# A hybrid decoder layer on one core: a smaller first load, products of ones at the start, a shorter last norm, and another order of work

## The chip, the cores and the metric

The kernel runs on one core of one Trainium2 chip. The metric is device time in microseconds (us); lower is better.

## The reference, cut to what matters

One layer (DEPTH 1), sequence 1024, width 1024, everything in float32. The normalised input goes through one projection to 5,648 columns; three mixers (SSD with 16 heads, HGRN2 with 4 heads, S5 with 32 groups) work on their parts; the three results are joined to 2,048 columns, projected back to 1,024, normalised and added to the input.

```python
h = rms_norm(x, pre_norm_w[l])
proj = h @ w_in[l]
z, xbc, dt_raw, q, f_raw, i_in, g, u, s5_gate = jnp.split(proj, splits, axis=-1)
y_ssd = ssd_mixer(z, xbc, dt_raw, ...)
y_hgrn = hgrn2_mixer(q, f_raw, i_in, g, lb_all[l], hgrn_norm_w[l])
y_s5 = s5_mixer(u, s5_gate, ...)
mix = jnp.concatenate([y_ssd, y_hgrn, y_s5], axis=-1).astype(x.dtype)
x = x + rms_norm(mix @ w_out[l], post_norm_w[l])
```

`rms_norm(y, w)` is `y * rsqrt(mean(y * y) + 1e-6) * w` over a row.

## The kernel before, in words

**Products.** Each float32 operand of a projection is split into a high part in float32r (an ACT copy) and a low part (a subtraction on DVE or POOL); `split` (L369) does both, and `mm3` (L373) makes three products of them. `c3(t)[:, k]` is the k-th block of 128 columns of a tile. A projection tile is 8 blocks x 2 halves of 512 columns x 3 products.

**The start.** `begin` (L445) projects the first two tiles, F0 and Q0, straight from the raw input: the norm's factor is multiplied in afterwards. It loads two weight tiles (`wr`, 128 x 1024) in halves and eight input blocks (`xs[k]`, 128 x 1024). For each block k ACT makes the high part `h`, scaled with column k of `prew`, DVE the low part `l` by a scalar_tensor_tensor; twelve products follow, six for each weight tile; ACT squares the block and DVE adds the square into `acc`. The weights are split in halves of 512 columns, at k = 0 and k = 4. Loads go out on two queues: `WQ` is ACT's, `S` is SyncE's (SP). After the last block two products with `ones` sum the squares, and `side_by_side` (L428) goes on with the next tiles while `normalise` (L507) rewrites `hh` and `hl`.

**The middle.** `PLAN` (L1531) is a string in which each letter emits one stage: `h` a head of HGRN2, `s` and `o` the two parts of an S5 batch, `c` a chunk of the SSD, `u x z a g v d` projections and preparations. The small products of the mixers write to four one-bank PSUM tiles (`c0` to `c3`, taken in turn by `bank()`), the projections mostly to two two-bank tiles (`p0`, `p1`).

**The end.** `s5_glu` (L1150) makes the S5 output and prepares half of the output weights `w_out` (`wout`, L851: an ACT copy scaled with `mix_w`, and a scalar_tensor_tensor on DVE); the eight others, into `r` tiles, follow at L1507. `out_prep` and `out_gate` load and gate a chunk of 128 rows, `out_split` (L1378) splits it into `v` tiles (ACT copy, DVE subtraction), `out_final` (L1385) multiplies with `w_out`, takes the row's sum of squares from an ACT Square with `accum_out`, corrects an approximate reciprocal root by one Newton step on 128 x 1 tiles (`y_`, `z_`, `v_`, `tot`), and writes chunk c. The last chunk is computed in three pieces of 512, 256 and 256 columns, whose sums are added.

**The order.** All instructions are recorded in a book. `Step` (L77) gives each a length in ns and a time after which others see its result (`post`); `depends` (L130) finds who must wait for whom; `arrange` (L169) is a list scheduler over the five engines with a model of the DMA bus (`BYTES` per ns, `TRIP`), of PE's slow clock and tile switches (`SWITCH`), of ACT's tables (`LOAD`) and of the port shared by DVE and POOL; among the ready instructions it takes the one that can start first, then the one of lowest rank, with a malus of `KEEP` for a change of tile kind or table. `improve` (L256) runs it forward and backward six times, each time with the start times of the run before as ranks, and keeps the shortest. `force` (L268) then fixes each engine's sequence, queues included.

Of the kernel before, what the change touches and what calls it, by code (L numbers as in the profile page):

```python
# [1 line left out]

# [13 lines left out]
P = 128  # L16
# [57 lines left out]
TABLES = {AF.Exp: 0, AF.Sigmoid: 1, AF.Silu: 2, AF.Gelu_apprx_tanh: 3, AF.Abs_reciprocal_sqrt: 4}  # L74


class Step:  # L77


    def __init__(self, i, ins):  # L80
        self.i, self.ins, self.mode, self.post, self.port = i, ins, None, 100.0, False
        self.eng = str(ins.engine).split(".")[-1]
        self.dma = ins.opcode == "DMACopy"
        if self.dma:
            o, x = ins.outs[0].bass_ap, ins.ins[0].bass_ap
            n = 1
            for _, c in o.ap:
                n *= int(c)
            run = min(int(y.ap[-1][1]) if int(y.ap[-1][0]) == 1 else 1 for y in (o, x))
            self.bytes = 4 * n / max(min(1.0, run * 4 / 512), 0.05)  # L90
            self.len = 60.0
        elif self.eng == "PE":
            n, t = size(ins.outs[0]), ins.tile_size[1]
            r = str(ins.ins[0].dtype).split(".")[-1] == "float32r"
            self.mode = t
            self.post = 200.0
            self.len = max(n / 2.4 + 14, 40) if r else 109.0 if ins.is_transpose else max(4 * n / 2.4 * t / P + 2, 15)
        else:
            n = max(size(x) for x in list(ins.outs) + list(ins.ins) if hasattr(x, "bass_ap"))
            srcs = [x.bass_ap for x in ins.ins if hasattr(x, "bass_ap")]  # L100
            self.post = 100.0
            if self.eng == "Activation":
                self.len = 140 + n / 1.2 + (80 if len(srcs) > 1 and n < 512 else 0)
                self.mode = TABLES.get(getattr(ins, "func", None))
            elif self.eng == "Pool":
                self.len = 50 + n / 1.15 if ins.opcode == "Memset" else 90 + 2.22 * n
                self.port = ins.opcode != "Memset"
            else:
                big = [x for x in srcs if size_of(x) > 1 or n == 1]
                self.port = not any(str(x.tensor.space) == "PSUM" for x in srcs)  # L110
                self.len = 95 + n / 0.96
                if ins.opcode == "Reciprocal":
                    self.len = 95 + 6.2 * n
                elif getattr(ins, "is_tensor_tensor_scan", False):
                    self.len += 105
                elif ins.opcode == "TensorScalarPtr" and len(big) > 1 and n > 32:
                    self.len += 55
                elif ins.opcode == "TensorScalarPtr" and self.port and n > 32:
                    self.len = 95 + n / 1.7


class Turn:

# [3 lines left out]
        self.i, self.behind = i, set()  # L127


def depends(book, places, rings, turns):  # L130

    steps = [Step(i, x) for i, x in enumerate(book)]
    ring = {n: f"{names[i % 2]} ring" for names in rings for i, n in enumerate(names)}
    banks = {x.bass_ap.tensor.name for b in book for x in b.outs if str(x.bass_ap.tensor.space) == "PSUM"}
    turn = [(set(x), set(y), Turn(len(book) + k)) for k, (x, y) in enumerate(turns)]
    seen = {}
    for s in steps:
# [15 lines left out]
        for (nm, c0, c1), w in ops:  # L155
# [2 lines left out]
                old[:] = [y for y in old if not (c0 <= y[0] and y[1] <= c1)]  # L158
            old.append((c0, c1, w, s.i))
        s.pre.discard(s.i)  # L160
    return steps + [x for *_, x in turn]


SWITCH, LOAD, BYTES, TRIP = 165.0, 1283.0, 255.0, 2000.0

STEP, KEEP, ROUNDS = 130.0, {"PE": 3000.0, "Activation": 3000.0}, 6


def arrange(steps, rank, back=False):  # L169
# [14 lines left out]
    engs = {s.eng: [] for s in steps if s.eng}  # L184
    now, mode, best = dict.fromkeys(engs, 0.0), dict.fromkeys(engs), dict.fromkeys(engs)
    order = {e: [] for e in engs}
    bus, cold, port = 0.0, 0.0, {"DVE": (0.0, 0.0), "Pool": (0.0, 0.0)}
    for s in steps:
        if not left[s.i] and s.eng:
            engs[s.eng].append(s.i)  # L190
# [11 lines left out]
    while any(engs.values()):  # L202
# [6 lines left out]
        order[e].append(i)  # L209
        start[i] = t  # L210
        if s.dma:
            bus = max(t + 1300, bus) + s.bytes / BYTES
            now[e] = t + s.len
            end = bus + TRIP - 1300
        else:
            n = s.len
            if e == "PE":
# [37 lines left out]

def improve(steps, rank):  # L256

    best = None
    for _ in range(ROUNDS):
        order, start, total = arrange(steps, rank)  # L260
        if best is None or total < best[1]:
            best = order, total
        _, start, _ = arrange(steps, start, True)
        rank = start
    return best[0]


def force(tc, steps, order):  # L268
# [8 lines left out]
def trunk(ctx: ExitStack, tc: tile.TileContext, a: dict, out: bass.AP, dbg=None):  # L277
# [124 lines left out]


    with tc.high_priority(offset=2 * PRI):
        prew = load_const("pre_w", [P, KD])
    ones = cst.tile([P, P], F32, tag="ones", name="ones")
    V.memset(ones, 1.0)
    eps = cst.tile([P, 1], F32, tag="eps", name="eps")
    V.memset(eps, EPS)
    warm = cst.tile([P, 1], F32, tag="warm", name="warm")  # L410
    A.copy(warm, ones[:, 0:1])
    hh, hl, xs = [], [], []

    def weights(src):

# [29 lines left out]
    def begin(ms):  # L445

        wr = [get("w") for m in ms]
        for w, m in zip(wr, ms):
            WQ.dma_start(w[:, HS[0]], a["w_in"][m][:, HS[0]])
        for k in range(KD):  # L450
            xs.append(slot())
            if k == 0:
                for n in range(2):
                    S.dma_start(xs[k][:, HS[n]], a["xT"][k][:, HS[n]])
            else:
                S.dma_start(xs[k], a["xT"][k])
            if k == 3:
                for w, m in zip(wr, ms):
                    S.dma_start(w[:, HS[1]], a["w_in"][m][:, HS[1]])
        ws = [[], []]  # L460
        ps = [pair(), pair()]
        acc = slot()
        for k in range(KD):
            h, l = get("r"), get("r")
            hf, i = k // 4, k % 4
            for t in range(2):
                if i == 0:
                    ws[t].append((get("v"), get("v")))
                    split(wr[t][:, HS[hf]], *ws[t][hf], V)
                if t == 0:  # L470
                    for s in HS if k == 0 else [slice(0, L)]:
# [913 lines left out]
    def out_final(c, y, hs, w, postw, parts=None):  # L1385
# [4 lines left out]
        if last:  # L1390
            pieces = [slice(0, 512), slice(512, 768), slice(768, 1024)]
            ps = [ps[0], ring("p")[:, 0:256], bank()[:, 0:256]]
        ms = small([P, 6], "ms")
        xr, o, junk = get("x"), get("x"), get("x")
        S.dma_start(xr, a["x"][c * P:(c + 1) * P, :])
        source, parts = parts or out_split(y, hs), []
# [8 lines left out]
        for i in range(4):  # L1405
            parts.append(next(source) if not isinstance(source, list) else source[i])
            if not last:
                for n in range(2):
                    product(i, n)
                free(*parts[i][:2])  # L1410
        y_, z_, v_ = ms[:, 0:1], ms[:, 1:2], ms[:, 2:3]
        tot = ms[:, 3:4]
        if last:
            for n, cols in enumerate(pieces):
                for i in range(4):
                    product(i, n)
                act(junk[:, cols], ps[n], AF.Square, accum_out=ms[:, 3 + n:4 + n])
                if n > 0:
                    add(V, tot, tot, ms[:, 3 + n:4 + n])
                if n < len(pieces) - 1:  # L1420
                    mul(V, o[:, cols], ps[n], postw[:, cols])
        else:
            act(junk, p, AF.Square, accum_out=tot)
        act(y_, tot, AF.Abs_reciprocal_sqrt, scale=1.0 / D, bias=eps)
        ts(V, v_, tot, 1.0 / D, ALU.mult, EPS, ALU.add)
        if last:
            mul(V, o[:, cols], ps[n], postw[:, cols])
        else:
            mul(V, o, p, postw)
        free(y, hs, junk)  # L1430
        mul(V, z_, y_, y_)
        stt(z_, z_, -0.5, v_, ALU.mult, ALU.mult)
        stt(y_, z_, 1.5, y_, ALU.add, ALU.mult)
        for s in pieces if last else [slice(0, L)]:
            stt(o[:, s], o[:, s], y_, xr[:, s], ALU.mult, ALU.add)
# [84 lines left out]
        parts = None  # L1520
    late_names = kept["s"] + kept["q"] + [postw.tensor.name]
    places = dict(zip(kept["m2"] + late_names, kept["y"] + kept["m"] + kept["y"]))
    steps = depends(book, places, rings.values(), [(kept["y"], kept["m2"]), (kept["m"] + kept["m2"], late_names)])
    force(tc, steps, improve(steps, [-STEP * s.ins.bass_priority if s.eng else 0.0 for s in steps]))


# [78 lines left out]
```

## Time and profile before

| what | us |
|---|---|
| median of 3 runs (lowest, highest) | 879.29 (878.73, 880.14) |
| the profiled execution | 878.0 |
| its span, first to last instruction | 876.2 |
| PE busy in the span | 854.7 |
| DVE, ACT, POOL busy in the span | 574.0, 396.5, 257.2 |

PE is TensorE's product row, PEld its weight loads, which run beside the products. DVE is VectorE, ACT ScalarE, POOL GpSimd, SP SyncE; a q behind a name means its queue, where transfers are issued. A product's end is modelled, so "busy" can hold short gaps: pace is read from the number of products in a stretch. The idle time before an instruction is put down to the event that came last.

### The profile page before, as it was taken

What the parts mean: (1) busy time and instruction counts of PE and PEld (TensorE: products, weight loads), DVE (VectorE), ACT (ScalarE), POOL (GpSimd) and SP (SyncE); (2) the same over time, 40 slices, a digit from 0 to 9 for tenths busy, and PEclk for the clock granted to TensorE, in tenths of its full rate; (3) what the DMA queues carried; (4) which work ended last, traced back from release to release, by engine and by line L of the source; (5) the groups of instructions that cost most, each with busy time, mean ns of one, the idle gap of its engine ahead of it and who ended that gap; (6) DMA issues with size and microseconds to landing.
All of it is one profiled execution on the core that took longest, in us unless ns stands there. A gap on an engine that the chain in (4) does not pass through costs nothing.

```text
span 876.2 us, 14850 instructions
## 1 busy us (share of the span) xinstructions
PE 854.7 (98%) x5857; PEld 704.9 (80%) x5857; DVE 574.0 (66%) x997; ACT 396.5 (45%) x627; POOL 257.2 (29%) x224
## 2 busy tenths in 40 slices
PE   7999999999999999999999999999999999999997
PEld 5789877789888888788888787877887778888886
DVE  6698389995748797767537353278656978555521
ACT  8465154562234525353257883773536732222210
POOL 0365032453233336234212243254113403111000
PEclk9999999999999999999999999999999999999999
DMA  7323012345233423356457595377866935343110
GB/s 269 92 63 133 2 49 74 97 149 150 59 97 83 140 86 109 83 139 202 147 168 227 179 341 165 114 235 231 274 198 166 327 122 190 132 133 132 61 49 25
DMA packets 91750, 124.67 MB, mean 142 GB/s; under 512 B 8416, under 2 KB 64416, under 8 KB 91680
## 3 DMA queue, kind: packets, MB, share of 16 engines
q1 hardware_dynamic: 80592, 99.01, 36.4%
q10 hardware_dynamic: 11088, 24.71, 9.7%
q8 instruction: 46, 0.75, 0.3%
q14 instruction: 24, 0.20, 0.1%
HBM read 89.52 MB, written 34.18 MB: 141 GB/s over the span
## 4 chain that ended last, share of the span: by engine, by line
PE 78%; DVE 12%; issue 3%; DMA 2%; ACT 2%; POOL 2%; SPq 0%; DVEq 0%; POOLq 0%; ACTq 0%
PE p L38 58%; PE c L38 20%; DVE m L38 7%; DVE x L38 2%; DVE h L38 1%; POOL v L38 1%; DMA m<-in_xT 1%; DMA x<-sm_d 1%; ACT r L38 1%; DVE r L38 1%; DVE s L38 1%; DMA w<-in_w_in 1%; DVE v L38 0%; DVE s5ph L38 0%; ACT x L38 0%
## 5 line engine op out<-in xcount | busy, mean ns | idle before, releaser
L38 PE MATMUL p<-r,v 128*128 128x512 f32 (+1 forms) x2208 | 536.0, 396 | 6.0 <-ACT r L38 5.9
L38 PEld LDWEIGHTS p<-r,v 128*128 128x128 f32 x2208 | 407.7, 189 | 93.3 <-issue 6.1
L38 POOL TENSOR_TENSOR v<-w,v 128x512 fp32r<-128x512 f32 x76 | 111.9, 1475 | 265.8 <-ACT v L38 204.8
L38 ACT ACTIVATE v<-w 128x512 fp32r<-128x512 f32 x88 | 54.5, 628 | 164.0 <-PE p L38 159.8
L38 DVE TENSOR_TENSOR m<-m,m 128x512 f32<-128x512 f32 (+8 forms) x114 | 106.2, 956 | 29.9 <-ACT m L38 15.0
L38 PE MATMUL p<-s,v 128*128 128x512 f32 (+1 forms) x384 | 88.8, 388 | 3.2 <-DVE v L38 3.2
L38 PEld LDWEIGHTS p<-s,v 128*128 128x128 f32 x384 | 70.3, 188 | 18.8 <-DVE v L38 4.5
L38 PEld LDWEIGHTS c<-m,m 128*32 128x32 f32 (+2 forms) x1904 | 61.2, 127 | 15.7 <-DVE m L38 7.8
L38 ACT ACT_TABLE_LOAD x53 | 68.0, 1283 | 11.7 <-DVE m L38 4.9
L38 PE MATMUL c<-m,m 128*32 128x16 f32 (+3 forms) x1904 | 66.4, 210 | 2.1 <-DVE m L38 2.0
L38 DVE SCALAR_TENSOR_TENSOR x<-p,conv_w,x 128x1023 f32<-128x1023 f32 (+2 forms) x36 | 46.0, 1277 | 8.5 <-ACT x L38 7.9
L38 PE MATMUL p<-y,r 128*128 128x272 f32 (+1 forms) x384 | 48.5, 286 | 0.8 <-DVE x L38 0.8
L38 PEld LDWEIGHTS p<-y,r 128*128 128x128 f32 x384 | 47.5, 190 | 1.3 <-ACT m L38 1.0
L38 ACT ACTIVATE m<-m,acol 128x128 f32<-128x128 f32 x128 | 40.0, 391 | 8.5 <-DMA m<-na_d 3.2
L38 PE MATMUL c<-s,s 128*128 128x512 f32 x192 | 43.7, 389 | 0.0
L38 PEld LDWEIGHTS c<-s,s 128*128 128x128 f32 x192 | 36.0, 188 | 7.5
L38 DVE TENSOR_TENSOR m<-m,sc 128x1024 f32<-128x1024 f32 x16 | 22.6, 1414 | 25.8 <-ACT m L38 25.3
L38 DVE TENSOR_TENSOR v<-x,v 128x512 fp32r<-128x512 f32 x20 | 15.6, 786 | 34.5 <-ACT v L38 34.5
L38 ACT ACTIVATE v<-x 128x512 fp32r<-128x512 f32 x20 | 12.4, 630 | 55.6 <-PE p L38 49.2
L38 POOL TENSOR_TENSOR h<-h 128x256 f32<-128x256 f32 (+1 forms) x12 | 10.6, 887 | 71.2 <-ACT h L38 50.2
L38 ACT COPY m<-c 128x512 f32<-128x512 f32 (+2 forms) x50 | 21.6, 446 | 19.2 <-PE c L38 19.0
L38 DVE SCALAR_TENSOR_TENSOR r<-m,pre_w,r 128x1024 fp32r<-128x1024 f32 (+1 forms) x17 | 26.4, 1561 | 1.6 <-ACT r L38 1.6
(195 smaller groups left out, 954.1 us busy)
## 6 DMA issues: line engine op xcount, KB each, us to landing
w<-in_w_in ACTq DMA_DIRECT2D x38, 512.0 KB, 3.9
m<-na_d SPq DMA_DIRECT2D x16, 512.0 KB, 5.1
xc_d<-x SPq DMA_DIRECT2D x12, 512.0 KB, 3.3
q<-in_w_out SPq DMA_DIRECT2D x12, 512.0 KB, 4.7
m<-tb_d SPq DMA_DIRECT2D x16, 256.0 KB, 4.5
m<-xc_d SPq DMA_DIRECT2D x8, 512.0 KB, 5.4
zc_d<-x SPq DMA_DIRECT2D x8, 512.0 KB, 5.4
ym_d<-m SPq DMA_DIRECT2D x8, 512.0 KB, 3.7
```

The source lines that it names most:

```text
L38: made = f(*args, **kw)
```

## The change

At the start, the two weight tiles are loaded in three pieces (columns 0 to 127 on ACT's queue, 128 to 511 after block 1, 512 to 1023 after block 3, both on SP's), and split at k = 0, 1 and 4. `prew` is loaded between the halves of the first block. Eight products of `ones` with `ones` (128 columns each, float32) are issued ahead of all others, into a bank that nobody reads. The instructions in `lead` keep their sequence on each queue. In the last norm the sum of the last piece stays by itself, and the two earlier sums go into the bias; y x y is joined with the next instruction, for all chunks. The planner's constants and its search change, so every engine's order may.

```diff
@@ -74,6 +75,10 @@
 TABLES = {AF.Exp: 0, AF.Sigmoid: 1, AF.Silu: 2, AF.Gelu_apprx_tanh: 3, AF.Abs_reciprocal_sqrt: 4}
+ROOM = {"PE": (1.0, 300.0), "DVE": (1.06, 200.0), "Activation": (1.05, 200.0), "Pool": (1.05, 200.0)}
 class Step:
@@ -87,8 +92,12 @@
             for _, c in o.ap:
                 n *= int(c)
             run = min(int(y.ap[-1][1]) if int(y.ap[-1][0]) == 1 else 1 for y in (o, x))
-            self.bytes = 4 * n / max(min(1.0, run * 4 / 512), 0.05)
-            self.len = 60.0
+            rows = max(1, min([int(y.ap[0][1]) for y in (o, x) if str(y.tensor.space) != "DRAM"] or [P]))
+            n *= 1.3 if rows == 64 else 1
+            n *= 1.5 if run < HALF or str(o.tensor.space) == "DRAM" else 1
+            self.bytes = 4 * n / max(min(1.0, run / P), 0.05)
+            self.len = 340.0
         elif self.eng == "PE":
             n, t = size(ins.outs[0]), ins.tile_size[1]
             r = str(ins.ins[0].dtype).split(".")[-1] == "float32r"
@@ -118,6 +127,11 @@
                 elif ins.opcode == "TensorScalarPtr" and self.port and n > 32:
                     self.len = 95 + n / 1.7
+        if not self.dma:
+            more, late = ROOM[self.eng]
+            self.len *= more
+            self.post += late
 class Turn:
@@ -127,11 +141,12 @@
         self.i, self.behind = i, set()
-def depends(book, places, rings, turns):
+def depends(book, places, rings, turns, lead=()):
     steps = [Step(i, x) for i, x in enumerate(book)]
+    at = {id(s.ins): s for s in steps}
     ring = {n: f"{names[i % 2]} ring" for names in rings for i, n in enumerate(names)}
     banks = {x.bass_ap.tensor.name for b in book for x in b.outs if str(x.bass_ap.tensor.space) == "PSUM"}
     turn = [(set(x), set(y), Turn(len(book) + k)) for k, (x, y) in enumerate(turns)]
@@ -158,12 +173,17 @@
                 old[:] = [y for y in old if not (c0 <= y[0] and y[1] <= c1)]
             old.append((c0, c1, w, s.i))
         s.pre.discard(s.i)
+    for q in {at[id(x)].eng for x in lead}:
+        line = [at[id(x)] for x in lead if at[id(x)].eng == q]
+        for x, y in zip(line, line[1:]):
+            y.behind.add(x.i)
     return steps + [x for *_, x in turn]
-SWITCH, LOAD, BYTES, TRIP = 165.0, 1283.0, 255.0, 2000.0
-STEP, KEEP, ROUNDS = 130.0, {"PE": 3000.0, "Activation": 3000.0}, 6
+SWITCH, LOAD, BYTES, TRIP, LANES = 165.0, 1283.0, 370.0, 2000.0, 8
+STEP, KEEP, ROUNDS, SEED, SHUFFLE = 130.0, {"PE": 3000.0, "Activation": 3000.0}, 2, 254, 1000.0
 def arrange(steps, rank, back=False):
@@ -184,7 +204,8 @@
     engs = {s.eng: [] for s in steps if s.eng}
     now, mode, best = dict.fromkeys(engs, 0.0), dict.fromkeys(engs), dict.fromkeys(engs)
     order = {e: [] for e in engs}
-    bus, cold, port = 0.0, 0.0, {"DVE": (0.0, 0.0), "Pool": (0.0, 0.0)}
+    bus, cold, lanes = 0.0, 0.0 if back else 3600.0, [0.0] * LANES
+    port = {"DVE": (0.0, 0.0), "Pool": (0.0, 0.0)}
     for s in steps:
         if not left[s.i] and s.eng:
             engs[s.eng].append(s.i)
@@ -209,9 +230,14 @@
         order[e].append(i)
         start[i] = t
         if s.dma:
+            if not back:
+                t = max(t, lanes[0])
+                start[i] = t
             bus = max(t + 1300, bus) + s.bytes / BYTES
             now[e] = t + s.len
             end = bus + TRIP - 1300
+            lanes = lanes[1:] + [end]
         else:
             n = s.len
             if e == "PE":
@@ -255,14 +281,12 @@
 def improve(steps, rank):
-    best = None
+    rng = random.Random(SEED)
+    rank = [r + rng.gauss(0, SHUFFLE) for r in rank]
     for _ in range(ROUNDS):
-        order, start, total = arrange(steps, rank)
-        if best is None or total < best[1]:
-            best = order, total
-        _, start, _ = arrange(steps, start, True)
-        rank = start
-    return best[0]
+        _, start, _ = arrange(steps, rank)
+        _, rank, _ = arrange(steps, start, True)
+    return arrange(steps, rank)[0]
 def force(tc, steps, order):
@@ -402,14 +426,19 @@
     with tc.high_priority(offset=2 * PRI):
-        prew = load_const("pre_w", [P, KD])
+        prew = cst.tile([P, KD], F32, tag="pre_w", name="pre_w")
     ones = cst.tile([P, P], F32, tag="ones", name="ones")
     V.memset(ones, 1.0)
     eps = cst.tile([P, 1], F32, tag="eps", name="eps")
     V.memset(eps, EPS)
     warm = cst.tile([P, 1], F32, tag="warm", name="warm")
     A.copy(warm, ones[:, 0:1])
-    hh, hl, xs = [], [], []
+    with tc.high_priority(offset=2 * PRI):
+        idle = bank()
+        for i in range(8):
+            T.matmul(idle[:, i % 4 * P:(i % 4 + 1) * P], ones, ones, start=True, stop=True)
+    hh, hl, xs, lead = [], [], [], []
     def weights(src):
@@ -445,18 +474,23 @@
     def begin(ms):
         wr = [get("w") for m in ms]
+        head, rest = slice(0, P), slice(P, HALF)
         for w, m in zip(wr, ms):
-            WQ.dma_start(w[:, HS[0]], a["w_in"][m][:, HS[0]])
+            lead.append(WQ.dma_start(w[:, head], a["w_in"][m][:, head]).ins)
         for k in range(KD):
             xs.append(slot())
             if k == 0:
-                for n in range(2):
-                    S.dma_start(xs[k][:, HS[n]], a["xT"][k][:, HS[n]])
+                lead.append(S.dma_start(xs[k][:, HS[0]], a["xT"][k][:, HS[0]]).ins)
+                lead.append(S.dma_start(prew, a["pre_w"]).ins)
+                lead.append(S.dma_start(xs[k][:, HS[1]], a["xT"][k][:, HS[1]]).ins)
             else:
-                S.dma_start(xs[k], a["xT"][k])
+                lead.append(S.dma_start(xs[k], a["xT"][k]).ins)
+            if k == 1:
+                for w, m in zip(wr, ms):
+                    lead.append(S.dma_start(w[:, rest], a["w_in"][m][:, rest]).ins)
             if k == 3:
                 for w, m in zip(wr, ms):
-                    S.dma_start(w[:, HS[1]], a["w_in"][m][:, HS[1]])
+                    lead.append(S.dma_start(w[:, HS[1]], a["w_in"][m][:, HS[1]]).ins)
         ws = [[], []]
         ps = [pair(), pair()]
         acc = slot()
@@ -466,6 +500,10 @@
             for t in range(2):
                 if i == 0:
                     ws[t].append((get("v"), get("v")))
+                if k < 2:
+                    cols = (head, rest)[k]
+                    split(wr[t][:, cols], *[x[:, cols] for x in ws[t][0]], V)
+                elif i == 0:
                     split(wr[t][:, HS[hf]], *ws[t][hf], V)
                 if t == 0:
                     for s in HS if k == 0 else [slice(0, L)]:
@@ -1390,7 +1428,7 @@
         if last:
             pieces = [slice(0, 512), slice(512, 768), slice(768, 1024)]
             ps = [ps[0], ring("p")[:, 0:256], bank()[:, 0:256]]
-        ms = small([P, 6], "ms")
+        ms = small([P, 8], "ms")
         xr, o, junk = get("x"), get("x"), get("x")
         S.dma_start(xr, a["x"][c * P:(c + 1) * P, :])
         source, parts = parts or out_split(y, hs), []
@@ -1408,28 +1446,31 @@
                 for n in range(2):
                     product(i, n)
                 free(*parts[i][:2])
-        y_, z_, v_ = ms[:, 0:1], ms[:, 1:2], ms[:, 2:3]
-        tot = ms[:, 3:4]
+        y_, z_, v_, tot = [ms[:, i:i + 1] for i in range(4)]
+        off, voff = eps, -0.5 * EPS
         if last:
             for n, cols in enumerate(pieces):
                 for i in range(4):
                     product(i, n)
-                act(junk[:, cols], ps[n], AF.Square, accum_out=ms[:, 3 + n:4 + n])
-                if n > 0:
-                    add(V, tot, tot, ms[:, 3 + n:4 + n])
+                act(junk[:, cols], ps[n], AF.Square, accum_out=tot if n == 2 else ms[:, 4 + n:5 + n])
+                if n == 1:
+                    off, voff = ms[:, 6:7], ms[:, 7:8]
+                    add(V, off, ms[:, 4:5], ms[:, 5:6])
+                    ts(V, off, off, 1.0 / D, ALU.mult, EPS, ALU.add)
+                    ts(V, voff, off, -0.5, ALU.mult)
                 if n < len(pieces) - 1:
                     mul(V, o[:, cols], ps[n], postw[:, cols])
         else:
             act(junk, p, AF.Square, accum_out=tot)
-        act(y_, tot, AF.Abs_reciprocal_sqrt, scale=1.0 / D, bias=eps)
-        ts(V, v_, tot, 1.0 / D, ALU.mult, EPS, ALU.add)
+        act(y_, tot, AF.Abs_reciprocal_sqrt, scale=1.0 / D, bias=off)
+        ts(V, v_, tot, -0.5 / D, ALU.mult, voff, ALU.add)
         if last:
             mul(V, o[:, cols], ps[n], postw[:, cols])
         else:
             mul(V, o, p, postw)
         free(y, hs, junk)
-        mul(V, z_, y_, y_)
-        stt(z_, z_, -0.5, v_, ALU.mult, ALU.mult)
+        stt(z_, y_, y_, v_, ALU.mult, ALU.mult)
         stt(y_, z_, 1.5, y_, ALU.add, ALU.mult)
         for s in pieces if last else [slice(0, L)]:
             stt(o[:, s], o[:, s], y_, xr[:, s], ALU.mult, ALU.add)
@@ -1520,7 +1561,7 @@
         parts = None
     late_names = kept["s"] + kept["q"] + [postw.tensor.name]
     places = dict(zip(kept["m2"] + late_names, kept["y"] + kept["m"] + kept["y"]))
-    steps = depends(book, places, rings.values(), [(kept["y"], kept["m2"]), (kept["m"] + kept["m2"], late_names)])
+    steps = depends(book, places, rings.values(), [(kept["y"], kept["m2"]), (kept["m"] + kept["m2"], late_names)], lead)
     force(tc, steps, improve(steps, [-STEP * s.ins.bass_priority if s.eng else 0.0 for s in steps]))
```

## Rows read from the trace of the kernel before

**Rows 1.** The page's first part: busy us (share of the span) and instructions of each engine.
```profile
PE 854.7 (98%) x5857; PEld 704.9 (80%) x5857; DVE 574.0 (66%) x997; ACT 396.5 (45%) x627; POOL 257.2 (29%) x224
```

**Rows 2.** Windows: length, busy (instructions) PE, PEld, DVE, ACT, POOL, granted clock, DMA share, GB/s.
```profile
5.90:10.00 4.10, 4.09 (x9) 3.15 (x10) 2.48 (x5) 3.69 (x5) 0.00 (x0) 1.00 1.00 402
10.00:30.00 20.00, 20.00 (x88) 16.42 (x87) 18.07 (x23) 14.86 (x18) 0.00 (x0) 1.00 0.60 188
30.00:660.00 630.00, 624.58 (x4821) 515.72 (x4821) 430.49 (x778) 306.02 (x488) 217.63 (x188) 1.00 0.47 141
...
680.00:700.00 20.00, 18.89 (x81) 14.70 (x80) 19.53 (x23) 15.35 (x19) 7.63 (x6) 1.00 0.94 323
700.00:720.00 20.00, 17.51 (x75) 13.90 (x76) 14.19 (x21) 6.00 (x11) 3.08 (x3) 1.00 0.35 122
...
870.00:876.20 6.20, 0.02 (x1) 0.00 (x0) 2.54 (x9) 0.77 (x3) 0.00 (x0) 0.83 0.24 85
```

**Rows 3.** The list of waits, PE alone: us in total, times, longest us.
```profile
PE p L38 <- ACT r L38: 5.9, 1, 5.9
PE c L38 <- DVE m L38: 3.9, 7, 1.0
PE p L38 <- DVE v L38: 3.2, 3, 1.9
```

**Rows 4.** Timeline of PE in the mixers: start us, us, engine, operation, count.
```profile
147.92 2.58 PE L38 MATMUL p<-r,v 128*128 128x512 f32 x10
150.43 0.73 PE L38 MATMUL c<-m,m 128*32 128x16 f32 x64
```

**Rows 5.** Timeline of the first 10 us: ones, the first two blocks, the loads.
```profile
0.83 0.17 DVE L38 MEMSET ones<- 128x128 f32 x1 [0.83 <-PEq L1597]
...
1.65 3.29 SPq L38 DMA_DIRECT2D m<-in_xT  x5
...
5.16 0.71 ACT L38 ACTIVATE r<-m,pre_w 128x512 fp32r<-128x512 f32 x1
...
8.35 1.15 ACT L38 ACTIVATE r<-m,pre_w 128x1024 fp32r<-128x1024 f32 x1 [0.41 <-DMA m<-in_xT]
...
9.53 1.28 DVE L38 SCALAR_TENSOR_TENSOR r<-m,pre_w,r 128x1024 fp32r<-128x1024 f32 x1 [1.62 <-ACT r L38]
```

**Rows 6.** DMA issues near 1.2, 2.1 and 2.5 us: count, KB each, us to landing.
```profile
w<-in_w_in ACTq DMA_DIRECT2D x1, 256.0 KB, 4.0
pre_w<-in_pre_w SPq DMA_DIRECT2D x1, 4.0 KB, 3.6
...
m<-in_xT SPq DMA_DIRECT2D x1, 512.0 KB, 6.2
...
m<-in_xT SPq DMA_DIRECT2D x1, 512.0 KB, 7.0
```

**Rows 7.** Groups by form in 0 to 30 us, ones products of the whole span: busy, mean ns.
```profile
L38 PE MATMUL p<-m,ones 128*128 128x512 f32 x4 | 1.9, 594 | 0.0
...
L38 DVE TENSOR_TENSOR v<-w,v 128x512 fp32r<-128x512 f32 x4 | 2.7, 684 | 4.3 <-ACT v L38 4.3
...
L38 ACT ACTIVATE v<-w 128x512 fp32r<-128x512 f32 x4 | 2.5, 619 | 1.5 <-DMA w<-in_w_in 1.5
```

**Rows 8.** Timeline around 700 us: DVE's subtractions, and PE after its longest wait there.
```profile
692.23 1.28 DVE L38 SCALAR_TENSOR_TENSOR r<-q,mix_w,r 128x1024 fp32r<-128x1024 f32 x1
...
693.42 0.68 DVE L38 TENSOR_TENSOR v<-x,v 128x512 fp32r<-128x512 f32 x1
...
701.82 5.28 PE L38 MATMUL p<-s,v 128*128 128x512 f32 x22 [1.92 <-DVE v L38]
```

**Rows 9.** Timeline after the last product: the norm of the last chunk on DVE.
```profile
870.56 0.16 DVE L38 TENSOR_TENSOR ms<-ms 128x1 f32<-128x1 f32 x1 [5.26 <-ACT q L38]
...
871.09 0.16 DVE L38 TENSOR_TENSOR ms<-ms 128x1 f32<-128x1 f32 x1
...
871.28 0.35 DVE L38 SCALAR_TENSOR_TENSOR ms<-ms 128x1 f32<-128x1 f32 x2
```

More of the change, by code (lines that the diff above doesn't have):

```diff
@@ L1 @@
+import random
 from contextlib import ExitStack
```

## The prediction

> **What bounds the kernel now.** I read the page's busy shares first: TensorE (PE) is busy for 854.7 of the 876.2 us span, and DVE, the next, for 574.0 [rows 1]. So 21.5 us of PE are idle. The windows and the waits say where: 5.9 us before the first product, 6.2 us after the last, which leaves 9.4 us in between; 5.4 us of it lie between 30 and 660 us and 3.6 us between 680 and 720 us [rows 2, 3]. The list of PE's waits names the releasers: one long wait for ACT at the start, then seven waits of about half a microsecond for DVE in the mixers, and three for a DVE split, 3.2 us together [rows 3].
>
> Two losses are not in that idle time. The first nine products take 4.09 us, 454 ns each; from 10 us on 88 take 20.00 us, 227 ns each [rows 2]. That is the ratio of TensorE's two levels, 1.2 and 2.4 GHz: the engine had done nothing before 5.9 us and the pace doubles near 10 us, though the granted clock reads 1.00 in both stretches. It costs 9 x 227 = 2.0 us. And each time PE goes from projections (512 columns) to the small mixer tiles and back, something is lost inside "busy": ten products between two small groups take 2.51 us from start to start, against 10 x 227 = 2.27 [rows 4], so 0.24 us a round trip.
>
> **The start.** Before, the first product waits for a 256 KB weight half (4.0 us to landing), its ACT copy, and then the ACT copy of the first half block, 5.16 to 5.87 [rows 5, 6]. The change cuts the two weight loads on ACT's queue to 128 columns (64 KB each), so 384 KB less stands ahead of the first blocks. Eight products of `ones` now go first on PE. Two 512-column ones products (two records each) took 1.9 us at the full pace [rows 7]; a quarter of the width at the half pace is 1.9/2/4 x 2 = 0.47 us, and eight are 3.8 us. `ones` is ready at 1.0 [rows 5], so they end near 4.9. They lie in time in which PE was idle; that cover is gone if the first half block is ready earlier than 4.9. With its landing 1.0 us earlier (below) its copy runs from 4.2 to 4.9, so I count nothing; whatever it comes before that is lost to them.
>
> The real work then starts at about 5.0 at the full pace. The ceiling of the gain is 0.9 + 2.0 = 2.9 us. It is not reached, because the second input block feeds PE next. It landed 6.2 us after its issue at about 2.1, which is when ACT took it (8.35), and DVE had its low part at 10.81 [rows 5, 6]; before, PE reached that block at 10.0 + 3 x 0.227 = 10.7, just as it was ready. With 384 KB less in front, at the 402 GB/s of that stretch [rows 2], it lands 1.0 us earlier. But the other 384 columns of both weight tiles now come behind it on SP's queue, and each needs an ACT copy and a DVE subtraction, bounded by the 512-column copy (0.62 us) and subtraction (0.68 us) [rows 7]. The third block has the same bytes ahead of it as before and lands near 9.5 (issued near 2.5, 7.0 us to landing [rows 6]); a copy of 1.15 us and a subtraction of 1.28 us [rows 5] put its low part at 12.0. Eleven of its twelve products follow: 12.0 + 11 x 0.227 = 14.5 us, against 10.0 + 27 x 0.227 = 16.1 before, 1.6 us. I take off 0.3 us for the two extra weight subtractions ahead of it on DVE: **a gain of 1.3 us**, between 0 (weights land as late as the third block, 9.5) and 2.9.
>
> On SP's queue two more transfers are issued ahead of block three, at the pace of five issues in 3.29 us [rows 5], and the second weight halves now pass block five: 512 KB, 1.3 us later for it, and 0.2 us for issues. That block is wanted at 18.9 (10.0 + 39 x 0.227). Block three landed at 9.5; two blocks more at 402 GB/s are 2.6 us, and the delay makes it 13.6, so with 1.15 and 1.28 us of copies there are still 2.9 us to spare. pre_w keeps its place behind the first half block. The dozen constants behind the blocks move by two issues, hidden: nobody reads them in the first 20 us. The bank that the ones products take turns the order of four banks by one; no price.
>
> A PE that waits for block two after the ones products could fall back to the lower level. The nearest row speaks against it: after a wait of 1.92 us at 699.9, 22 products took 5.28 us, 240 ns each [rows 8]. The Trainium skill ("TensorE: Matmul & The Clock Gate", Part 1) has idle time lower the clock again, and has the moment of the rise vary between runs; by the worst of it the 2.0 us is not gained, and the start would give nothing, which is counted in rival B. No run here shows that yet.
>
> **The order.** The planner gets new lengths (other engines 5 to 6% slower, results seen 200 to 300 ns later, DMA issues 340 ns instead of 60, at most eight transfers in flight, a slow clock at the start) and starts from jittered ranks with another pick of rounds. It removes and adds no work; each engine's list is the same, in another sequence. A later visibility of results makes it put more PE work between a producer and its reader, which is what the short waits want. Of the 9.4 us the 3.2 for the split stay, as DVE is full there (19.53 of 20 us from 680 on [rows 2]); of the other 6.2 I take half, **3 us**, between all of it and none. The bounds are a gain of 9.4 us (all idle in between) and, on the other side, a loss by the last rival's price with all eight w_out subtractions, 10.2 us. The count of round trips between tile kinds I leave as it is, since the price that the planner puts on a switch is unchanged; twenty more or fewer would be 5 us either way, inside these bounds.
>
> **The tail.** Before, after the last Square, DVE adds the last sum (0.16 us at 870.56), for which ACT's rsqrt waits, and a product y x y at 871.09 stands ahead of the two corrections at 871.28 [rows 9]. The change takes the sum of the first two pieces into the bias, earlier, while PE computes, and joins y x y into the next instruction. That takes from the chain half the add, as DVE's next instruction overlaps it, 0.08, and the product's 0.19 us (871.09 to 871.28): **0.3 us**; bounds 0 and 0.35. In the seven other chunks the saved instruction lies beside PE work.
>
> **Sum.** 878.0 (profiled execution, span 876.2 and 1.8 around it) - 1.3 - 3.0 - 0.3 = 873.4. The median of the runs is 879.29, 1.3 above the profiled one: 873.4 + 1.3 = **874.7 us**.
>
> **Rivals.**
> A. All idle time in between goes: 878.0 - 1.3 - 9.4 - 0.3 + 1.3 = 868.3 us. For it: PE depends on DVE, which is idle a third of the span [rows 1]. Against it: the full DVE from 680 us on; no order makes it faster there.
>
> B. The start gives nothing and the new order is as good as the old: 878.0 - 0.3 + 1.3 = 879.0 us. The first copy is scaled with pre_w, 4 KB, which took 3.6 us from its issue near 1.2 [rows 6], about as long as the 256 KB halves; if it lands at 4.8 again, the first product comes at 5.5, and late weight columns take the rest. The Trainium skill ("DMA: Bandwidth & Descriptors", Anatomy of one DMA) agrees that most of a small transfer's time is fixed, about 2 us. By that the smaller weight load alone would save 0.4 us at 436 GB/s, an estimate from the page. This rival also holds the case that the new lengths change little in the order.
>
> C. Slower: the order hurts between 680 and 720 us. DVE is full there, and the w_out subtractions (r, 1.28 us each) stand among the splits (v, 0.68 us) for which PE waits: at 693.42 a split starts only when the one of 692.23 is through [rows 8]. If the new ranks put six of the eight further ahead of the splits, PE waits 6 x 1.28 = 7.7 us more: 874.7 + 7.7 = 882.4. It decides from four on, where it has eaten the whole gain of 4.6 us. For it: the new lengths make DVE work look longer and thus more urgent. Against it: a planner that sees PE's end as its goal should not.
>
> **How the numbers follow.** What a measurement can tell from no change is about 0.2%, 1.8 us, so faster is below 877.5 and slower above 881.0. The forecast gets 0.47 (its own range 871.5 to 877.5), A 0.17, B 0.16, C 0.20. Forecast and A are faster, 0.64; B is the same, 0.16; C is slower, 0.20. The range 867 to 883 takes in the bounds of the start and the tail, most of A, B, and C up to six subtractions; it leaves out some 0.06 below and 0.1 above.
>
> **What would show it.** At the start: small ones products from about 1.1 to 4.9 us, the first real product near 5.0, 227 ns apart from the beginning, a gap before the second block, and the first phase's 96 products ending 1.3 us earlier than 10.0 + 87 x 0.227 = 29.7. In the middle: PE idle of 6 to 7 us, with shorter waits for DVE m. At 680 to 720 us: waits for v no longer than 3.2 us in all. At the end: no add after the last Square, and 5.9 us from the last product to the end. Wrong would be a first product still past 5.5 us, half-pace products after 6 us, or PE idle in between of more than 10 us; more round trips between tile kinds would show as the same idle time with a longer busy time.

## The result and the profile after

The changed kernel takes 865.59 us (863.14 to 867.70), the kernel before 879.01 (877.30 to 880.14): a ratio of 0.9848 with a 95% interval of 0.9813 to 0.9883. The forecast was 874.7, in a range of 867 to 883: the sign was right, the gain three times as large. The profiled execution took 864.15 us, 13.9 less than that of before.

The page's first part of the changed kernel, and its windows (columns as in [rows 2]):

```profile
PE 852.2 (99%) x5873; PEld 708.9 (82%) x5873; DVE 580.0 (67%) x992; ACT 395.2 (46%) x627; POOL 254.0 (29%) x224
```

```profile
5.26:6.70 1.44, 1.44 (x3) 1.07 (x4) 1.40 (x2) 1.44 (x2) 0.00 (x0) 1.00 0.98 318
6.70:8.10 1.40, 1.40 (x7) 1.14 (x6) 0.07 (x1) 1.32 (x3) 0.00 (x0) 1.00 1.03 363
...
30.00:660.00 630.00, 629.63 (x4861) 524.54 (x4860) 449.09 (x794) 309.68 (x494) 215.42 (x191) 1.00 0.49 146
...
680.00:700.00 20.00, 18.07 (x79) 14.34 (x78) 18.07 (x23) 9.44 (x13) 3.74 (x3) 1.00 0.78 271
700.00:720.00 20.00, 20.00 (x90) 16.56 (x89) 15.46 (x26) 6.63 (x12) 3.16 (x3) 1.00 0.50 165
```

The ones products add 3.8 us of busy time that does no work. Counted as idle, PE's idle time goes from 21.5 to 862.3 - 852.2 + 3.8 = 13.9 us, 7.6 less, and its useful busy time from 854.7 to 848.4, 6.3 less. Of the latter about 2 us are the slow first products. The rest, some 4 us, are mainly stalls that stood inside "busy": PE goes from one kind of tile to another 96 times instead of 98, which at the prediction's 0.24 us for two changes is only 0.2 us. Between 30 and 660 us the idle time went from 5.4 to 0.4 us.

Where stalls hide in busy time, the row of weight loads shows them. Its list of waits (us in total, times, longest), 30 to 660 us, before:

```profile
PEld c L38 <- DVE m L38: 12.5, 23, 1.4
...
PEld c L38 <- ACT m L38: 2.4, 9, 0.4
PEld p L38 <- ACT m L38: 1.2, 2, 1.0
```

and after:

```profile
PEld c L39 <- DVE m L39: 3.4, 8, 0.8
...
PEld c L39 <- ACT m L39: 0.4, 1, 0.4
```

The waits for ACT's m went from 3.6 to 0.4 us, those for DVE's from 12.5 to 3.4; all waits of the weight loads for another engine in this stretch came to 21.4 us before and 6.6 after. For DVE's m PE's products had shown 3.9 us [rows 3]. A product's modelled end covers part of each wait; the load that stands in front of it does not. Not every microsecond of these waits is lost: they fell by 14.8 us, and the whole order, idle time included, gained less (12.3, below).

PE's own waits after the change, and the timeline of the start (the second wait is that of the ones products for DVE's memsets):

```profile
PE p L39 <- ACT v L39: 1.9, 2, 1.6
PE c L39 <- DVE eps L39: 1.1, 1, 1.1
```

```profile
1.05 3.79 PE L39 MATMUL c<-ones 128*128 128x128 f32 x16 [1.05 <-DVE eps L39]
...
5.26 7.12 PE L39 MATMUL p<-r,v 128*128 128x512 f32 x26 [0.42 <-ACT r L39]
...
28.64 0.84 PE L39 MATMUL c<-r,v 128*128 128x512 f32 x3
29.32 1.88 PE L39 MATMUL p<-m,ones 128*128 128x512 f32 x4
```

The ones products run from 1.05 to 4.84, and the first real product comes at 5.26. Three products still come at half pace (1.44 us), then seven in 1.40 us. The first phase's last product gives way to the next tile at 28.64. Before, the phase ended where its sum of squares began:

```profile
30.03 1.89 PE L38 MATMUL p<-m,ones 128*128 128x512 f32 x4
```

That is 1.4 us earlier. The tail, on DVE after the last product (856.28; before, 870.02), answers to [rows 9]; its last step is the scaling into x:

```profile
856.82 0.42 DVE L39 TENSOR_TENSOR x<-c,postw 128x256 f32<-128x256 f32 x1 [4.64 <-ACT q L39]
...
857.47 0.41 DVE L39 SCALAR_TENSOR_TENSOR ms<-ms 128x1 f32<-128x1 f32 x2
857.92 1.54 DVE L39 SCALAR_TENSOR_TENSOR x<-x,ms,x 128x512 f32<-128x512 f32 x3
```

and before:

```profile
871.67 1.54 DVE L38 SCALAR_TENSOR_TENSOR x<-x,ms,x 128x512 f32<-128x512 f32 x3
```

The add and the product are gone, and yet the scaling begins as long after the last product as before (1.64 against 1.65 us). From the last product to the end it takes 6.1 us instead of 6.2. So some 12.3 of the 13.9 us lie between the first phase and the tail: in the order.

### The profile page after: what moved, and what is told of

Same layout as the page of the kernel before. It is cut to its first block, busy times and chain, and to the rows that moved or that the text cites. A ratio compares the mean times of both kernels' runs of the same rounds, so it can differ in the third digit from the quotient of the medians.

```text
span 862.3 us, 14892 instructions
## 1 busy us (share of the span) xinstructions
PE 852.2 (99%) x5873; PEld 708.9 (82%) x5873; DVE 580.0 (67%) x992; ACT 395.2 (46%) x627; POOL 254.0 (29%) x224
## 4 chain that ended last, share of the span: by engine, by line
PE 92%; DVE 4%; DMA 2%; issue 1%; ACT 0%; SPq 0%; DVEq 0%
PE p L39 69%; PE c L39 23%; DVE m L39 2%; DVE h L39 1%; DMA h<-zc_d 1%; DMA w<-in_w_out 1%; DMA q<-in_w_out 1%; DMA m<-in_xT 1%; DVE r L39 0%; DVE x L39 0%; DVE s L39 0%; DVE s5cis L39 0%; SPq L39 0%; DVE v L39 0%; ACT r L39 0%
## 5 line engine op out<-in xcount | busy, mean ns | idle before, releaser
L39 POOL TENSOR_TENSOR v<-w,v 128x512 fp32r<-128x512 f32 x76 | 110.0, 1450 | 242.5 <-ACT v L39 206.2
L39 ACT ACTIVATE v<-w 128x512 fp32r<-128x512 f32 (+2 forms) x90 | 55.5, 621 | 181.9 <-PE p L39 163.8
L39 DVE TENSOR_TENSOR m<-m,sc 128x1024 f32<-128x1024 f32 x16 | 23.2, 1448 | 14.3 <-ACT m L39 13.8
L39 ACT COPY m<-c 128x512 f32<-128x512 f32 (+2 forms) x50 | 21.5, 450 | 18.2 <-PE c L39 17.9
L39 DVE TENSOR_TENSOR h<-c,m 128x512 f32<-128x512 f32 x8 | 5.5, 684 | 34.8 <-PE c L39 24.2
L39 DVE SCALAR_TENSOR_TENSOR m<-m,ssd_d,c 128x128 f32<-128x128 f32 x64 | 18.2, 343 | 14.7 <-PE c L39 14.6
```

The source lines that it names most:

```text
L39: made = f(*args, **kw)
```

## The experiments

Two theories stood against each other: the start's and the tail's gain pass through and the planner's later visibility of results does the rest (slack), or it matters which of many shuffled orders was taken (the draw).

**The start and the norm alone.** The planner's lengths, transfer model and search are put back:

```diff
-ROOM = {"PE": (1.0, 300.0), "DVE": (1.06, 200.0), ...}
+ROOM = {"PE": (1.0, 0.0), "DVE": (1.0, 0.0), ...}
...
-            self.len = 340.0
...
+            self.len = 60.0
...
-SWITCH, LOAD, BYTES, TRIP, LANES = 165.0, 1283.0, 370.0, 2000.0, 8
...
+SWITCH, LOAD, BYTES, TRIP, LANES = 165.0, 1283.0, 255.0, 2000.0, 100000
...
-    bus, cold, lanes = 0.0, 0.0 if back else 3600.0, [0.0] * LANES
+    bus, cold, lanes = 0.0, 0.0, [0.0] * LANES
...
-    rank = [r + rng.gauss(0, SHUFFLE) for r in rank]
     for _ in range(ROUNDS):
-        _, start, _ = arrange(steps, rank)
-        _, rank, _ = arrange(steps, start, True)
-    return arrange(steps, rank)[0]
+        order, start, total = arrange(steps, rank)
+        if best is None or total < best[1]:
+            best = order, total
...
+    return best[0]
```

> The changed start and last norm, under the planner of before (its lengths, its six rounds, no shuffle). Mine (the start and the tail give what they gave in the changed kernel, 1.4 and 0.2 us, and the order gives the rest): 1.6 us under the kernel before, near 877.5. Rival (the start lets the whole chain slide earlier and so brings most of the 13.4 us): below 870.

Measured: 878.8 us, ratio 0.9996 (0.9986 to 1.0007). Neither: no gain at all. The first phase ended 0.6 us earlier (the sum's products at 29.41 instead of 30.03), but by the output stage 0.2 us was left, and there the same wait for a split came, with another end. PE's timeline, and two windows of one microsecond:

```profile
701.62 6.90 PE L39 MATMUL p<-s,v 128*128 128x512 f32 x22 [1.92 <-DVE v L39]
```

```profile
702.00:703.00 1.00, 1.00 (x3) 0.75 (x3) 1.00 (x2) 0.00 (x0) 0.00 (x0) 0.50 0.43 109
...
706.00:707.00 1.00, 1.00 (x7) 0.79 (x6) 0.97 (x2) 0.60 (x1) 0.00 (x0) 1.00 0.22 90
```

The same 22 products after the same wait of 1.92 us took 5.28 us before [rows 8] and 6.90 here: the granted clock was 0.50, the level of 1.2 GHz. That is 1.6 us for a wait that looked alike.

**The order alone.** The start and the norm of before under the new planner, seed 254:

```diff
-            T.matmul(idle[:, i % 4 * P:(i % 4 + 1) * P], ones, ones, start=True, stop=True)
...
-            lead.append(WQ.dma_start(w[:, head], a["w_in"][m][:, head]).ins)
+            WQ.dma_start(w[:, HS[0]], a["w_in"][m][:, HS[0]])
...
-        act(y_, tot, AF.Abs_reciprocal_sqrt, scale=1.0 / D, bias=off)
+        act(y_, tot, AF.Abs_reciprocal_sqrt, scale=1.0 / D, bias=eps)
```

> The start and the norm of before, under the new planner with its seed and constants. Mine: some 11 to 12 us under the kernel before, near 867 to 868, with weight-load waits for DVE, ACT and POOL between 30 and 660 us of 5 to 10 us instead of 21. Rival: the draw was picked for the changed program, and another program with the same seed gets an ordinary order: 873 to 879.

Measured: 873.18 us, 0.9931 (0.9912 to 0.9950). The rival's number: half the gain. The weight-load waits between 30 and 660 us came to 11.3 us, a little more than expected. The parts do not add up (0 and 6 us alone, 13.4 together): the same seed makes another order of another program. One wait there shows the price of the clock again; 87 products of 256 columns stand behind it, six a microsecond and then eleven:

```profile
207.85 1.11 PE L39 MATMUL c<-ident,m 128*128 128x128 f32 x4 [2.98 <-DVE dte__1567 L39]
208.62 13.01 PE L39 MATMUL p<-y,r 128*128 128x256 f32 x87
```

```profile
208.00:209.00 1.00, 1.00 (x6) 1.00 (x7) 0.31 (x3) 0.98 (x3) 0.00 (x0) 0.50 1.03 311
...
214.00:215.00 1.00, 1.00 (x11) 1.00 (x10) 0.00 (x0) 0.00 (x0) 0.00 (x0) 1.00 1.09 327
```

**Allowances out, other draws.** In the changed kernel, one constant each:

```diff
-ROOM = {"PE": (1.0, 300.0), ...}
+ROOM = {"PE": (1.0, 0.0), ...}
```

> The changed kernel, but the planner's allowances taken out (other engines 5 to 6% longer, results 200 to 300 ns later). Theory of slack: the short waits come back, 6 us or more slower than the changed kernel, 872 or above. Theory of the draw (which shuffle it is matters, not the allowance): like any other shuffle, and the next run tells what that is. Theory of the DMA model: no more than 3 us slower.

Measured: 884.0 us, 1.0056 (1.0036 to 1.0076).

```diff
-STEP, KEEP, ROUNDS, SEED, SHUFFLE = 130.0, {...}, 2, 254, 1000.0
+STEP, KEEP, ROUNDS, SEED, SHUFFLE = 130.0, {...}, 2, 1, 1000.0
```

> The changed kernel with seed 1 in place of 254, all else the same. Theory of slack: within 3 us of the changed kernel, below 869. Theory of the draw: 5 us or more slower, above 871.

Measured: 873.42 us, 0.9934 (0.9917 to 0.9951). Both above the changed kernel, so the draw counts for some 8 us, and the first result could be either theory's.

> The changed kernel with the ranks not jittered at all (spread 0), allowances and the rest kept. After the runs before this one (taking the allowances out: 18 us slower; seed 1: 8 us slower): the allowance moves the whole field, the seed picks within it. Then this is an ordinary draw of the field with allowances: 870 to 877. If instead the jitter itself did harm that only a lucky seed repairs: below 868.

(`SHUFFLE = 0.0`.) Measured: 884.74 us, 1.0070 (1.0050 to 1.0090), slower than said.

> The changed kernel with seed 2. Field with allowances: 870 to 877, as seed 1 gave 873.4. Rival (seed 254 is not special and seed 1 was bad luck): below 869.

(`SEED = 2`.) Measured: 882.66 us, 1.0046 (1.0030 to 1.0062), again slower: the field is wider than two draws had shown.

> Allowances out, seed 1: a second draw of the field without allowances. If the allowance moves the field: 879 to 887, at least 6 us above seed 1 with them (873.4). Rival (884 with seed 254 was one bad draw): 871 to 876.

(`ROOM` neutral and `SEED = 1`.) Measured: 874.2 us, 0.9955 (0.9940 to 0.9970). The rival's number: without allowances two draws gave 884.0 and 874.2, with them 873.4, 882.7 and 884.7. The allowance does not shift the field of times in these draws; slack, as I had put it, falls. What the allowance does do shows further down.

> The changed kernel, but transfers are modelled as before (60 ns an issue, 255 bytes per ns, no limit in flight). If the DMA model matters little: an ordinary draw of the field, 870 to 877. If it carries the gain: above 879, with PE waits that end in transfers.

(`self.bytes`, `self.len`, `BYTES` and `LANES` as before.) Measured: 887.94 us, 1.0112 (1.0094 to 1.0130), with 11.8 us of waits for an ACT copy of v. That this is the model and not just another draw, one run can't say.

**Luck, or foreseen?** Run over a fixed sequence, the planner's own model gives an end for each draw. It can be set beside the span of the profiled execution:

```
draw                            model    span
seed 254 (the change)           860.1    862.3
seed 1                          867.5    871.5
seed 2                          876.2    879.5
no shuffle                      883.7    882.3
no allowances, seed 1           855.1    873.6   (model without allowances too)
no allowances, seed 254         859.1    881.6   (model without allowances too)
2800 seeds with allowances: best 858.8, one tenth below 867.7, median 877.7
30 seeds without allowances: all between 855.1 and 864.5
```

Three seeds were then chosen by the model, with its numbers said first.

> The changed kernel with seed 36. The planner's own model (its lengths, run over the fixed sequence) says 889.7 us for it, where it says 860.1 for seed 254, 867.5 for seed 1 and 876.2 for seed 2. Theory (the quality of an order can be foreseen by this model, and the picking uses it): 888 to 897, the slowest of the seeds run. Rival (luck: the model cannot tell draws apart on the chip): like the other draws, 872 to 885.

Measured: 890.91 us, 1.0142 (1.0123 to 1.0162), span 888.9 for a model's 889.7.

> The changed kernel with seed 24: the model says 866.1 us, 873.6 on lengths jittered by 4%. Theory: 868 to 875, between seed 254 and seed 2. Rival (luck): anywhere from 865 to 888.

Measured: 870.09 us, 0.9909 (0.9885 to 0.9932), span 867.8 for 866.1.

> The changed kernel with seed 1326: of 2800 seeds the one that the model puts best on jittered lengths (859.1 us, 862.0 jittered; seed 254 has 860.1 and 862.6). Theory: as fast as the changed kernel within 2 us, 862 to 866, and clearly under every other draw. Rival (luck): 872 to 885.

Measured: 864.11 us, 0.9835 (0.9816 to 0.9854), span 862.5 for 859.1. It equals the changed kernel and does not beat it. All three fell where the model had put them. So the draw decides, and what it gives can be foreseen: with the allowances the model's end is within 4 us of the span for all eight orders that were planned with this model, and a search over shuffles can find the good orders. (The eighth order is that of the order alone: 872.0 by the model, a span of 872.6.) How seed 254 was found is not on record; the model puts it 12th of the 2800.

The model is no general forecast, though. Run over the sequences of the kernel before and of the two planned without allowances, the model with allowances gives 921.4, 916.7 and 912.0 us, where the spans were 876.2, 881.6 and 873.6: it fits the orders that were made to keep its allowances, and not these three. Without the allowances the model gives nearly the same end to every draw and misses by 18 to 23 us; how well a search with it would pick, two draws can't say.

The traces show what the draws differ in. The weight-load waits between 30 and 660 us come to 17.1 to 21.4 us in the four kernels planned without allowances (before, the start alone, and the two with the allowances out), and to 6.6 to 14.1 us in the nine planned with them, those above 880 us too. So the short waits do give way to the allowance. What the draws above 880 us lose, they lose by a few long ones. PE's waits of 1 us and more, behind its first real product, come to 1.6 us in the changed kernel and none with seed 1326, but to 12.0 with seed 2, 13.8 without shuffle and 19.4 with seed 36. Between the first and the last product the granted clock is 0.50 for 17, 10 and 27 us in these three, and never in the other two.

**What is left: a wait on ACT, and the ones products.** The changed kernel once more, on the chip of the two runs that follow:

> The changed kernel once more, beside the two that follow. Its four runs gave 863.1, 864.2, 867.0 and 867.7. If the spread is TensorE falling to its lower level after the waits of up to 1.6 us near 682 us in some runs and not in others: again values near 863 and near 867, and the granted clock lower in the latter.

Measured: 864.32 us (863.80 to 864.79), 0.9837 (0.9820 to 0.9854). No values near 867 this time. The earlier 867.03 and 867.70 came with a mean granted clock of 0.997, the 863.14 and 864.15 beside them with 0.998 and 0.999, so the clock fell in them as supposed; at which wait stays open, as no trace of them is kept. The repeat shows one thing more: its first phase ended 0.7 us later than in the first profiled execution, and its span is the same (862.4 and 862.3 us).

In the next, ACT's copies to v tiles pass the w_out copies that wait for their transfers:

```diff
+def pass_splits(steps, line, held):
...
+    for i in [i for i in line if id(steps[i].ins) in held]:
+        n = line.index(i)
+        while n + 1 < len(line) and is_split(steps[line[n + 1]]) and i not in steps[line[n + 1]].pre:
+            line[n], line[n + 1] = line[n + 1], line[n]
+            n += 1
```

> The changed kernel, with one thing moved on ACT: copies to v tiles that stand right behind a w_out copy go ahead of it. In the changed kernel two of those w_out copies wait for their transfers (1.37 and 0.63 us) with the v copies, for which PE waits 0.36 and 1.57 us, behind them. Mine: the wait of 1.57 us goes to 0.3 or less, 862 to 863, and the runs near 867 are gone. Rival (DVE or another load is late next): PE waits as long for a v subtraction, no change.

Measured: 863.77 us, 0.9829 (0.9812 to 0.9847), not to be told from the run beside it. The wait of 1.5 us near 684 us is gone, as expected, and the gain is not there. Another wait came at 544 us, for DVE's h; the one for ACT's v that is left lies in the first phase. PE's waits:

```profile
PE c L39 <- DVE h L39: 1.1, 1, 1.1
...
PE p L39 <- ACT v L39: 0.5, 1, 0.5
```

Last, the ones products at one column (`ones[:, 0:1]`), with a length in the planner that keeps every engine's sequence:

> The changed kernel with the eight ones products one column wide instead of 128; all engines keep their sequence. Tells what the ones products are worth. By the prediction's term: half pace until about 9 us, the first 96 products end 0.3 to 1.0 us later (they wait for blocks two and three anyway), and the time is less than 1 us longer. Rival (the whole cold loss comes back): 2 us longer.

Measured: 864.65 us, 0.9855 (0.9830 to 0.9880): the same. Windows of the start, first this kernel, then the changed one beside it:

```profile
5.30:9.00 3.70, 3.70 (x9) 2.83 (x10) 1.47 (x3) 2.75 (x4) 0.00 (x0) 1.00 0.98 343
9.00:13.00 4.00, 4.00 (x17) 3.26 (x16) 4.00 (x5) 4.00 (x6) 0.00 (x0) 1.00 1.03 411
```

```profile
5.30:9.00 3.70, 3.34 (x12) 2.02 (x12) 1.83 (x3) 3.18 (x5) 0.00 (x0) 1.00 1.01 374
9.00:13.00 4.00, 3.90 (x14) 2.47 (x14) 4.00 (x5) 4.00 (x6) 0.00 (x0) 1.00 1.03 410
```

Nine products against twelve in the first stretch, then 17 against 14: the slow start is made up while the quick one waits for blocks. The sum of squares begins at 30.28 against 29.98, 0.3 us later, where two executions of the changed kernel differ by 0.7 (29.32 and 29.98). So what the ones products are worth is too little to be told here. The narrow products still loaded 128 columns of weights each, for 3.5 us in all, and that did not raise the pace of the products behind them.

## Why the prediction was wrong

**The start: right in size, with some luck.** Forecast 1.3 us, measured 1.4 in the profiled execution and 0.7 in the repeat (29.30, where the next tile's first product stood at 28.64). The first real product came at 5.26 (forecast 5.0), and the second and third block set the end, as the sum had it: PE waited for the third one's low part until 12.64 (forecast 12.0). The pace was not full from the first product on, though the sum had it so: three came at half pace. And start and order do not add: under the old planner the 0.6 us of the start were gone by the output stage, and the repeat lost 0.7 us of it without ending later.

**The tail: wrong, and small.** Forecast 0.3, measured 0.1, and none of that from the shorter norm. The add and the product y x y were not what held it: DVE's product with `postw` and the step behind it end 1.1 us after the last product in both kernels, and the scaling begins at 1.64 and 1.65.

**The order: the step that failed.** Of 9.4 us idle in between, 3.2 were to stay, and "of the other 6.2 I take half, 3 us". It measured 12.3. Four things were wrong with it. The stalls were read from PE's products, 9.4 us between the first product and the last; the list of weight-load waits would have shown that more was hidden in busy time (12.5 us for one releaser that I counted with 3.9). I named the cost of a tile switch for it, 0.24 us a round trip, which had next to nothing to do with it (98 changes of tile kind before, 96 after). The 3.2 us for the DVE split did not stay: PE waited for no DVE split after 680 us, and 1.9 us for ACT's. And I asked what the new allowances do to the order, when the question was what a pick among many orders gives. One order drawn at random from this planner would about as likely have been a loss as a gain: the median of 2800 seeds is 877.7 by the model, near the span of before. The best tenth lies 10 us lower, and the change takes one of the very best. I priced one draw, where seed 254 is one of the best among many.

**The rivals.** A, all idle time in between gone (868.3), was nearest and still too slow, since it left the hidden stalls alone: idle in between went from 9.4 to 2.6 us, and some 5 us more of the 12.3 came out of busy time. What stood against it, the full DVE from 680 us on, did not hold: an order made it better there. B and C did not happen. pre_w, which B had late again, landed 2.9 us after its issue instead of 3.6, and PE's idle time between 680 and 720 us went from 3.6 to 1.9 us.

**The clock.** I took one row [rows 8] as evidence that a wait of 1.9 us leaves TensorE at 2.4 GHz. The same wait did not under the changed start and the old planner (granted clock 0.50).

## What to carry to other kernels

Where a planner makes the order, ask first how well its forecast fits the chip. Without allowances it gave every order nearly the same good number; with them it fitted the orders that it had planned itself, though not three others, and a pick among shuffles was worth 10 us and more. Read stalls from the weight loads, not from the products alone. A gain at the start counts only if no later wait takes it back; run the part alone before adding it up. Where one execution shows a gain of 1 us somewhere, look at a second one of the same kernel.

## What was not expected of the hardware

A wait of TensorE costs more than its length, at times. After 1.92 us without work it went on at 2.4 GHz in one kernel [rows 8] and at 1.2 GHz (granted clock 0.50) in another, at a cost of 1.6 us. The kernel before goes both ways from one execution to the next: of its eleven beside the last three kernels, the five with a mean granted clock of 0.996 or 0.997 took 879.2 to 880.5 us, the six with 0.998 or 0.999 took 877.1 to 877.9. After 2.98 us it went on at 1.2 GHz, from 208 to past 213 us. The draws with long times have more of this: the mean granted clock of their profiled executions is 0.984 (seed 36), 0.989 (seed 2), 0.990 (old transfer model) and 0.993 (no shuffle, and no allowances with seed 254), against 0.999 in the changed kernel. Seed 36, the slowest, waited 5.0, 7.4 and 1.0 us between 682 and 702 us, and its 22 products after that took 7.46 us:

```profile
687.77 4.28 PE L39 MATMUL c<-h,ones 128*128 128x512 f32 x4 [5.03 <-POOL h L39]
699.45 1.22 PE L39 MATMUL p<-s,v 128*128 128x512 f32 x2 [7.41 <-ACT v L39]
701.62 7.46 PE L39 MATMUL p<-s,v 128*128 128x512 f32 x22 [0.95 <-DVE v L39]
```

The Trainium skill ("TensorE: Matmul & The Clock Gate", Part 1) says that idle time lowers the clock and that the moment of its rise varies between runs. These runs agree with both: behind the same ones products three products came at half pace in the changed kernel (1.44 us) and eight with seed 1326 (3.55 us). They show besides that a wait of one length can go either way. At the very start the granted clock reads 1.00 while the products run at half pace [rows 2], so the pace, not that column, tells the level there.
